# Hybrid encoder, two layers on one core: VectorE's waits for GpSimd counted for small operands, three projections in lockstep, memory keys 512 wide

## The chip, the core and the metric

The kernel runs on one NeuronCore of a Trainium2 chip. The metric is the time of one execution in microseconds (us) as the device reports it. Five engines work side by side, each with its own queue of instructions in fixed order: TensorE (PE in the profile, its weight loads PEld) multiplies matrices and writes PSUM; VectorE (DVE), ScalarE (ACT) and GpSimd (POOL) work on elements; SyncE (SP) issues most of the DMAs. An instruction waits on semaphores for what it needs, and all that stands behind it on its engine waits with it.

## The reference

An encoder of two layers over 512 tokens of width 1024, all in float32 (batch 1). Cut to what matters:

```python
for l in range(2):
    x = x + hybrid_mixer(rms_norm(x, norm_mix[l]), w_in[l], ...)      # 8 neighbourhood heads and 8 grouped-query heads
    x = x + memory_cross_attention(rms_norm(x, norm_mem_q[l]),        # 4 heads of width 128 over 256 memory tokens
                                   rms_norm(mem, norm_mem_kv[l]), ...)
    x = x + conv_ffn(rms_norm(x, norm_ffn[l]), ...)                   # 2 x 2816 wide, convolution of width 3, SwiGLU
return rms_norm(x, norm_final)
```

The mixer's one input projection gives queries, keys and values of both kinds of heads. In the grouped-query heads queries and keys are normalised per head, so the scores of a query are scaled by a factor of its own before the softmax. The memory keys are `rms_norm(mem) @ w_k`, 256 tokens by 512 columns, a product of its own in each layer.

## The kernel before

**Precision.** Every float32 operand of a matmul is kept as two parts, `hi` (rounded, by a copy on ScalarE) and `lo` (the difference, by a subtraction on GpSimd for weights or VectorE for activations). A product is three matmuls: hi by hi, hi by lo, lo by hi (`mm3`, line 609; `gemm_T`, 615). Norms are applied late: the operand is x times the gain, and the factor of each token is multiplied in after the projection.

**Tiles.** x lies transposed: `xT[0..7]` (line 621), eight tiles of 128 features by 512 tokens, 2048 bytes a row. Gains, convolution weights and biases lie in `par` (622). Weights come by DMA into `raw`, two buffers (`N_RAW`), or into the pool of 21 buffers tagged `r` where the plan says so (`"Dx"`, line 576); they are split into `hi` and `lo`, four buffers each. PSUM has eight banks: four tagged `mm` for projections, two `sc` for scores, two `tr` for transposes and small sums.

**The order of the work.** The function `encoder_kernel` doesn't issue anything itself. `Taped` engines record each call as a `Step` (line 73) on a `Tape`, with a cost from `Step.times`, the steps it needs, and whether it is `shared`, that is whether the model lets it and GpSimd's instructions exclude each other (line 97). `Tape.touch` notes for every tile who must wait for whom; line 178 makes each user of a tile need the tile's first user. `Tape.plan` (323) runs a list scheduler several times with three margins (`PLANS`), reckons due times backwards (`due`, 202), replays each order with random delays, and keeps the order with the best mean. `play` issues that order. In `run` (227) a shared step on VectorE is lengthened until the port is free (lines 293 to 296). Before the change a VectorE step is shared if it reads at least two operands of more than 16 columns and none of them lies in PSUM. All instructions are issued in `play`, so the profile gives line 355 for nearly everything; tiles tell them apart.

**Start.** `FIRST` (line 627) lists the first loads: x's chunks (integers) and pieces `(u, k0, k1)` of the first three projections' weights (u = 0, 1, 2; chunks k0 to k1), in pieces of two or four chunks. The eight gains of the first norm come as a DMA of their own on ScalarE's queue (628). `Norm.operand` (691) makes `hi` and `lo` of x times gain. `project_first` (853) then multiplies in an order that mixes the three projections, with the first two chunks of two of them written out by hand (864). The rest of `par` is loaded by `load_parameters` (644), after the projections.

**Grouped-query scores.** `gqa_scores` (1162) takes 128 queries of two heads. Per head j: two matmuls into a bank `sc`; VectorE reduces the row maximum, negated, into one column of `nmx`; VectorE multiplies it by the query's factor, one column `gr` (line 1173); ScalarE computes the exponential with that column as bias; GpSimd normalises; TensorE transposes. In the profile these are `s<-sc` (reduce), `s<-s,s` (multiply), `t<-sc,s,s` (exponential), `sc<-r,r` (scores). Only two banks hold scores, so a late exponential holds back the scores after the next. Projections, output products and the memory's keys and values are woven between as fillers (`attn_fill`, 1308).

**Memory keys.** `memory_prepare` (761) makes, for each of eight chunks of the memory, `hi` and `lo` of 256 columns, which lie side by side in a tile `mg`. `memory_keys` (1273) runs per head eight chunks of three matmuls of 256 columns into one half of a bank, then VectorE multiplies out of PSUM by `mem_rep` (the tokens' factors) into `u`, and `hi` and `lo` of that are made.

Of the kernel before, what the change touches and what calls it, by code (L numbers as in the profile page):

```python
# [19 lines left out]
P = 128  # L20
# [36 lines left out]
IN_PSUM = ("mm", "sc", "tr")  # L57
ASIDE = {"mm": 1, "r": 9, "t": 9, "s": 9}
# [14 lines left out]
class Step:  # L73
# [3 lines left out]
                 "opens", "tiles")  # L77

    def __init__(self, i, engine, name, call, args, kwargs):
        self.i, self.engine, self.name, self.call = i, engine, name, (call, args, kwargs)  # L80
        self.reads, self.writes = [], []
        for n, a in [*enumerate(args), *kwargs.items()]:
            if hasattr(a, "tensor") or type(a).__name__ == "Tile":
                a = a if hasattr(a, "ap") and not callable(a.ap) else a[:]
                (self.writes if n in (0, "out", "accum_out") else self.reads).append(a)
        self.needs, self.frees, self.opens, self.tiles, self.moved = set(), set(), [], [], 0
# [60 lines left out]
class Tape:  # L147
# [6 lines left out]
    def take(self, engine, name, call, args, kwargs):  # L154
        s = Step(len(self.steps), engine, name, call, args, kwargs)
        for a, w in [(a, False) for a in s.reads] + [(a, True) for a in s.writes]:
            if type(a.tensor).__name__ == "Tile":
                self.touch(s, a, w)
        s.needs.discard(s.i)
        for x in s.needs:  # L160
            self.steps[x].frees.add(s.i)
        self.steps.append(s)

    def touch(self, s, a, writes):
# [37 lines left out]
    def due(self, start, rank):  # L202

        later = [[] for _ in self.steps]
        for tag, tiles in self.opened.items():
            tiles = sorted(tiles, key=lambda t: rank[self.users[t][0]])
            for a, b in zip(tiles, tiles[self.bufs.get(tag, len(tiles)) :]):
                first = self.users[b][0]
                for x in self.users[a]:
                    if rank[x] < rank[first]:  # L210
                        later[x].append(first)
        at, now = [0.0] * len(self.steps), 0.0
        by_rank = sorted(self.steps, key=lambda s: rank[s.i])
        for s in by_rank:
            if s.engine == E_PE:
                now = start[s.i]
            at[s.i] = now + 30000.0 * (s.engine != E_PE)
        for s in reversed(by_rank):
            long = HANDOVER + (s.busy + LANDING + s.moved / BYTES_PER_NS if s.moved else s.length)
            for x in s.frees:  # L220
                same = self.steps[x].engine == s.engine and not s.moved
                at[s.i] = min(at[s.i], at[x] - (s.busy if same else long))
            for x in later[s.i]:
                at[s.i] = min(at[s.i], at[x] - long)
        return at

    def run(self, due, rank, patience, ahead, margin=0.0, aside={}, order=None, rng=None):
# [3 lines left out]
        todo = [len(s.needs) for s in steps]  # L231
# [28 lines left out]
        for _ in steps:  # L260
# [53 lines left out]
            for x in s.frees:  # L314
# [4 lines left out]
                if not todo[x]:  # L319
                    open_to[q.engine].append(x)  # L320
        return max(start), start, taken
# [128 lines left out]
def encoder_kernel(ctx: ExitStack, tc: tile.TileContext, t: dict, out: bass.AP):  # L450
# [170 lines left out]
    xT = [xpool.tile([P, S], F32, tag=f"x{c}", name=f"xT{c}") for c in range(KC)]  # L621
# [5 lines left out]
    FIRST = [0, (0, 0, 2), 1, (1, 0, 2), 2, (0, 2, 4), 3, (1, 2, 4), (2, 0, 4), 4, (0, 4, 8), 5, (1, 4, 8), (2, 4, 8), 6, 7]  # L627
    ACT.dma_start(par[:, 0, 0:8], t["par"][:, 0, 0:8])
    first_loads = []
    for n in FIRST:  # L630
        if isinstance(n, int):
            SP.dma_start(xT[n], t["xT"][n * P : (n + 1) * P, :])
            continue
        u, k0, k1 = n
# [3 lines left out]
        (ACT if u < 2 and k0 == 0 else SP).dma_start(raw[:, k0:k1], loads[0][1][:, k0:k1])  # L638
# [35 lines left out]
    class Norm:  # L674
# [16 lines left out]
        def operand(self, c, act=ACT, src=None, dve=DVE, hi_only=False, lo_only=False):  # L691
            src = xT[c] if src is None else src
            g = par[:, self.l, self.gcol + c : self.gcol + c + 1]
# [65 lines left out]
    mops = []  # L759

    def memory_prepare(l):

        mops.clear()
        raw = load_mem()
        yield
        for c in range(KC):
# [7 lines left out]
            mops.append((hi, lo))  # L774
            if c % 2 == 1:
                yield
# [38 lines left out]
    for n in FIRST:  # L815
# [3 lines left out]
        u, k0, k1 = n  # L819
        if u == len(ready):  # L820
            if plan[u][4][1:] == "r":
                ready.append((rtile((KC, P)), rtile((KC, P))))
            else:
                ready.append(tuple(wpool.tile([P, KC, P], F32R, tag=tag, name=nm(tag)) for tag in ("hi", "lo")))
        raw, (hi, lo) = raws[u], ready[u]
        k = slice(k0, k1)
# [7 lines left out]
        if k1 == KC:  # L834
# [6 lines left out]
    for l in range(DEPTH):  # L841
# [11 lines left out]
        def project_first():  # L853

            w, pms = {}, {}
            for u, k0, k1 in ((0, 0, 2), (1, 0, 2), (0, 2, 4), (1, 2, 4), (2, 0, 4), (0, 4, 6),
                              (1, 4, 6), (2, 4, 6), (0, 6, 8), (1, 6, 8), (2, 6, 8)):
                if u not in w:
                    w[u], pms[u] = get_w(NA_ORDER[u]), ps_s() if u < 2 else ps_mm()
                if (u, k0) == (0, 0):  # L860
                    continue
                if (u, k0) == (1, 0):

                    for v, a, b, k in ((0, 0, 0, 0), (0, 1, 0, 0), (0, 0, 0, 1), (0, 0, 1, 0), (1, 0, 0, 0), (1, 0, 0, 1),
                                       (0, 1, 0, 1), (0, 0, 1, 1), (1, 0, 1, 0), (1, 0, 1, 1), (1, 1, 0, 0), (1, 1, 0, 1)):
                        PE.matmul(pms[v], w[v][a][:, k], xg[k][b], start=(a, b, k) == (0, 0, 0), stop=False)
                    continue
                gemm_T(pms[u], w[u], xg, range(k0, k1), 0, KC - 1)
# [293 lines left out]
        def gqa_scores(u):  # L1162
# [110 lines left out]
        def memory_keys():  # L1273
            yield lambda: len(mops) == KC
            for h in range(4):
# [392 lines left out]
```

## Time and profile before

| | |
|---|---|
| timed runs, median of 3 | 1354.14 us (1353.62 to 1354.2) |
| profiled execution, whole | 1354.9 us |
| its span, first to last instruction | 1353.1 us |
| mean granted TensorE clock | 0.995 |
| instructions in the span | 18192 |
| HBM read, written | 125.65 MB, 2.10 MB |

A line of a group reads: source line, engine, operation, tiles written and read, shapes, count; then busy time in us, mean ns of one, idle time of the engine just before them, and after `<-` what ended it. In a timeline a row has start and length in us, and in square brackets the idle time before and its releaser. A row of the stages has the stretch, its length, the busy time and count of each engine, the granted clock, the DMA share and GB/s. A row of a tile has the count and the least, median and greatest duration in ns.

### The profile page before, as it was taken

Reading aid. Unit: us, or ns where it says so; the run is one execution under the profiler, and the core shown is the slowest. Engines: PE = TensorE matmul, PEld = TensorE weight load, DVE = VectorE, ACT = ScalarE, POOL = GpSimd, SP = SyncE. Lnnn points to the kernel's source line nnn. Section 1 sums busy time; section 2 is a strip of 40 time slices with the busy share of each in tenths; the row PEclk is TensorE's granted clock in tenths of the full one; section 3 lists DMA queues with packets and bytes.
Section 4 is the critical chain, followed back from the end, with each engine's and each line's share of the span. In section 5 each row is a group of like instructions: output and inputs, shape, how many; then the busy total and the mean of one; then the engine's idle time right before and its main releaser. Section 6 shows DMA issues by size and latency. Waiting matters only on the chain.

```text
span 1353.1 us, 18192 instructions
## 1 busy us (share of the span) xinstructions
PE 1332.5 (98%) x6620; PEld 1120.9 (83%) x6620; DVE 941.4 (70%) x1609; ACT 679.6 (50%) x1230; POOL 686.5 (51%) x475
## 2 busy tenths in 40 slices
PE   8999999999999999999999999999999999999997
PEld 7898788888888888888888987888888888888897
DVE  5679985676995388178435898856769925853884
ACT  6676676555443244233447767755634423432441
POOL 2474865727445444443636655756454544444451
PEclk9999999999999999999999999999999999999998
DMA  7761312323333332333265422133133333333331
GB/s 245 185 180 48 94 49 77 94 62 94 108 95 93 100 103 82 105 118 92 81 170 156 144 75 63 63 79 108 49 107 96 93 104 99 91 97 98 100 84 63
DMA packets 204504, 136.78 MB, mean 101 GB/s; under 512 B 5248, under 2 KB 193024, under 8 KB 204416
## 3 DMA queue, kind: packets, MB, share of 16 engines
q1 hardware_dynamic: 203312, 134.97, 34.2%
q8 instruction: 52, 0.85, 0.2%
q10 hardware_dynamic: 1104, 0.66, 0.2%
q14 instruction: 36, 0.29, 0.1%
HBM read 125.65 MB, written 2.10 MB: 94 GB/s over the span
## 4 chain that ended last, share of the span: by engine, by line
PE 88%; DVE 8%; ACT 2%; DMA 1%; issue 1%; POOL 0%; ACTq 0%; DVEq 0%
PE mm L355 79%; PE sc L355 5%; PE tr L355 4%; DVE s L355 3%; DVE t L355 2%; DVE r L355 1%; ACT t L355 1%; DVE xg L355 1%; DMA r<-r 0%; DVE xT L355 0%; ACT r L355 0%; DMA par<-in_par 0%; DVE sc L355 0%; DVE mm L355 0%; ACT xg L355 0%
## 5 line engine op out<-in xcount | busy, mean ns | idle before, releaser
L355 POOL TENSOR_TENSOR lo<-raw,hi 128x1024 fp32r<-128x1024 f32 (+2 forms) x268 | 506.8, 1902 | 505.9 <-ACT hi L355 467.8
L355 PE MATMUL mm<-xg,hi 128*128 128x512 f32 x1728 | 535.1, 390 | 0.0
L355 ACT CAST hi<-raw 128x512 fp32r<-128x512 f32 (+3 forms) x281 | 228.4, 831 | 313.4 <-PE mm L355 282.5
L355 PEld LDWEIGHTS mm<-xg,hi 128*128 128x128 f32 x1728 | 322.4, 188 | 65.2
L355 PE MATMUL mm<-xg,lo 128*128 128x512 f32 x864 | 336.4, 389 | 0.0
L355 PE MATMUL mm<-r,hi 128*128 128x512 f32 (+1 forms) x1144 | 333.8, 374 | 0.1
L355 DVE SCALAR_TENSOR_TENSOR t<-t,par,t 128x504 f32<-128x504 f32 (+1 forms) x352 | 247.7, 739 | 35.9 <-ACT t L355 32.2
L355 PEld LDWEIGHTS mm<-r,hi 128*128 128x128 f32 x1144 | 209.8, 189 | 38.7 <-DVE r L355 0.3
L355 PE MATMUL mm<-r,lo 128*128 128x512 f32 (+1 forms) x572 | 213.6, 373 | 0.0
L355 PEld LDWEIGHTS mm<-xg,lo 128*128 128x128 f32 x864 | 162.2, 188 | 33.7
L355 PEld LDWEIGHTS mm<-r,lo 128*128 128x128 f32 x572 | 107.8, 188 | 18.7
L355 DVE TENSOR_TENSOR xT<-xT,mm 128x512 f32<-128x512 f32 (+1 forms) x64 | 39.4, 618 | 118.3 <-PE mm L355 118.2
L355 PE MATMUL mm<-hi,xg 128*128 128x512 f32 (+1 forms) x384 | 107.9, 357 | 0.0
L355 POOL TENSOR_SCALAR t<-t,s 128x512 f32<-128x512 f32 (+1 forms) x112 | 67.6, 619 | 77.6 <-DVE s L355 70.9
L355 ACT ACTIVATE t<-sc,s,s 128x512 f32<-128x512 f32 (+1 forms) x96 | 67.9, 709 | 41.5 <-DVE s L355 41.2
L355 DVE TENSOR_TENSOR t<-mm,rep 128x512 f32<-128x512 f32 x88 | 60.0, 686 | 37.6 <-PE mm L355 22.3
L355 PE MATMUL sc<-r,r 128*128 128x256 f32 (+1 forms) x352 | 80.5, 341 | 5.6 <-ACT t L355 4.8
L355 ACT ACTIVATE t<-t,par 128x512 f32<-128x512 f32 x88 | 71.6, 814 | 28.0 <-DVE t L355 28.0
L355 DVE TENSOR_TENSOR t<-t,t 128x512 f32<-128x512 f32 (+1 forms) x68 | 76.4, 1123 | 8.6 <-ACT t L355 4.4
L355 DVE TENSOR_TENSOR r<-t,r 128x512 fp32r<-128x512 f32 (+1 forms) x52 | 71.5, 1375 | 13.5 <-ACT r L355 12.5
L355 PEld LDWEIGHTS mm<-hi,xg 128*128 128x128 f32 x384 | 68.6, 189 | 9.4
L355 PE MATMUL tr<-ident,t 128*128 128x128 f32 x488 | 70.8, 274 | 3.1 <-DVE r L355 1.6
(111 smaller groups left out, 1531.9 us busy)
## 6 DMA issues: line engine op xcount, KB each, us to landing
raw<-in_w_up SPq DMA_DIRECT2D x88, 512.0 KB, 3.8
raw<-in_w_in SPq DMA_DIRECT2D x33, 512.0 KB, 4.5
raw<-in_w_down SPq DMA_DIRECT2D x32, 448.0 KB, 3.8
raw<-in_w_mem_kv SPq DMA_DIRECT2D x16, 512.0 KB, 3.6
raw<-in_w_down SPq DMA_DIRECT2D x16, 512.0 KB, 4.0
r<-r SPq DMA_DIRECT2D x30, 256.0 KB, 3.6
r<-in_bias SPq DMA_DIRECT2D x16, 384.0 KB, 5.9
raw<-in_w_out SPq DMA_DIRECT2D x8, 512.0 KB, 3.3
```

Source lines behind the costliest of these rows:

```text
L355: call(*args, **kwargs)
```

## The change

Seven edits, in the order of the diff:

- `shared` on VectorE is no longer decided by width. Operations with two tensor inputs (`TWO_INPUTS`) are shared if their first and last input lie in SBUF, whatever their width; `tensor_scalar` and `tensor_copy` (`FAST`) are shared if they write more than four columns and both input and output lie in SBUF.
- Users of a tile that don't need the first user's data come after it in the order (`after`, `leads`) without waiting for its end.
- The first three projections all keep their raw weights in the `r` pool.
- x's chunks become 513 columns wide in the input and in SBUF; column 512 holds the first layer's first gain. The DMA of eight gains goes away, and `par` is loaded whole, in one DMA, after the projections.
- `FIRST` takes the weights in pieces of two chunks of all three projections, and `project_first` multiplies chunk by chunk, the three projections in turn.
- The one-column multiply of `gqa_scores` becomes a `tensor_scalar` that multiplies by the column and by 1.0.
- The memory keys' hi by hi and hi by lo become one matmul of 512 columns into both halves of a bank, lo by hi one of 256 into the first half; VectorE then copies the second half to SBUF, adds the first half, and multiplies by `mem_rep`.

Beside these, the reserve in SBUF for dynamic DMA is set to 1024 bytes. The diff, cut to its core:

```diff
+TWO_INPUTS = ("tensor_add", "tensor_sub", "tensor_mul", "tensor_tensor", "scalar_tensor_tensor")
+FAST = ("tensor_scalar", "tensor_copy")
...
-        wide = [a for a in self.reads if columns(a) > 16]
+        ends = self.reads[:: max(1, len(self.reads) - 1)] if name in TWO_INPUTS else self.reads[:1] + self.writes
         self.shared = engine == E_POOL or (
-            engine == E_DVE and len(wide) > 1 and all(tag_of(a.tensor) not in IN_PSUM for a in wide))
+            engine == E_DVE and (name in TWO_INPUTS or name in FAST and columns(self.writes[0]) > 4)
+            and all(tag_of(a.tensor) not in IN_PSUM for a in ends))
...
-            s.needs.add(self.users[t.name][0])
+            s.after.add(self.users[t.name][0])
...
+            for x in s.leads:
+                ready[x] = max(ready[x], t)
+                todo[x] -= 1
+                if not todo[x]:
+                    open_to[steps[x].engine].append(x)
...
-                eng = {("q", 0): "D", ("k", 0): "D", ("q", 1): "Dx"}.get((n, p), "P") if l == 0 else "P"
+                eng = {("q", 0): "Dx", ("k", 0): "Dx", ("q", 1): "Dx"}.get((n, p), "P") if l == 0 else "P"
...
-    xT = [xpool.tile([P, S], F32, tag=f"x{c}", name=f"xT{c}") for c in range(KC)]
+    xg0 = [xpool.tile([P, S + 1], F32, tag=f"x{c}", name=f"xT{c}") for c in range(KC)]
+    xT = [x[:, 0:S] for x in xg0]
...
-    FIRST = [0, (0, 0, 2), 1, (1, 0, 2), 2, (0, 2, 4), 3, (1, 2, 4), (2, 0, 4), 4, (0, 4, 8), 5, (1, 4, 8), (2, 4, 8), 6, 7]
-    ACT.dma_start(par[:, 0, 0:8], t["par"][:, 0, 0:8])
+    FIRST = [0, (0, 0), (1, 0), (2, 0), 1, 2, (0, 2), (1, 2), (2, 2), 3, 4, (0, 4), (1, 4), (2, 4), 5, 6, (0, 6), (1, 6), (2, 6), 7]
...
-        SP.dma_start(par[:, 0, 8:], t["par"][:, 0, 8:])
-        SP.dma_start(par[:, 1], t["par"][:, 1])
+        SP.dma_start(par, t["par"])
...
+            w = [get_w(NA_ORDER[u]) for u in range(3)]
+            pms = [ps_s(), ps_s(), ps_mm()]
+            for k in range(KC):
+                for u in range(3):
+                    gemm_T(pms[u], w[u], xg, [k], 0, KC - 1)
...
-                DVE.tensor_mul(nmx[:, c], nmx[:, c], gr[b][:, h])
+                DVE.tensor_scalar(nmx[:, c], nmx[:, c], gr[b][:, h], 1.0, op0=ALU.mult, op1=ALU.mult)
...
-                pm = ps_mm()[:, :MEMN]
-                w = get_w(("memk", h))
-                gemm_T(pm, w, mops, range(0, 4), 0, KC - 1)
-                yield
-                gemm_T(pm, w, mops, range(4, 8), 0, KC - 1)
+                pm = ps_mm().rearrange("p (n m) -> p n m", n=2)
+                wh, wl = get_w(("memk", h))
+                for k in range(KC):
+                    PE.matmul(pm, wh[:, k], both[k], start=k == 0, stop=False)
+                    PE.matmul(pm[:, 0], wl[:, k], mops[k][0], start=False, stop=k == KC - 1)
+                    if k == 3:
+                        yield
                 u = tmp((MEMN,))
-                DVE.tensor_mul(u, pm, mem_rep)
+                DVE.tensor_copy(u, pm[:, 1])
+                DVE.tensor_add(u, pm[:, 0], u)
+                DVE.tensor_mul(u, u, mem_rep)
...
-    nc = bacc.Bacc("TRN2", target_bir_lowering=False, num_devices=1)
+    nc = bacc.Bacc("TRN2", target_bir_lowering=False, num_devices=1, dynamic_dma_scratch_size=1024)
```

More of the change, by code (lines that the diff above doesn't have):

```diff
@@ L76 @@
     __slots__ = ("i", "engine", "name", "call", "reads", "writes", "busy", "length", "moved", "shared", "needs", "frees",
-                 "opens", "tiles")
+                 "after", "leads", "opens", "tiles")
     def __init__(self, i, engine, name, call, args, kwargs):
@@ L159, in take @@
         s.needs.discard(s.i)
+        s.after -= s.needs | {s.i}
         for x in s.needs:
             self.steps[x].frees.add(s.i)
+        for x in s.after:
+            self.steps[x].leads.add(s.i)
         self.steps.append(s)
@@ L230, in run @@
         steps = self.steps
-        todo = [len(s.needs) for s in steps]
+        todo = [len(s.needs) + len(s.after) for s in steps]
         start, ready, free = [-1.0] * len(steps), [0.0] * len(steps), [0.0] * 5
@@ L637, in encoder_kernel @@
         raw, loads = first_loads[u]
-        (ACT if u < 2 and k0 == 0 else SP).dma_start(raw[:, k0:k1], loads[0][1][:, k0:k1])
+        (ACT if u < 2 and k0 == 0 else SP).dma_start(raw[:, k0 : k0 + 2], loads[0][1][:, k0 : k0 + 2])
     ACT.copy(small(1), ones)
@@ L818, in encoder_kernel @@
             continue
-        u, k0, k1 = n
+        u, k0 = n
         if u == len(ready):
[L821 to L824, printed above, removed]
+            ready.append(tuple(wpool.tile([P, KC, P], F32R, tag=tag, name=nm(tag)) for tag in ("hi", "lo")))
         raw, (hi, lo) = raws[u], ready[u]
-        k = slice(k0, k1)
+        k = slice(k0, k0 + 2)
         if (u, k0) == (0, 0):
```

32 lines of the change are left out of this document (12 added, 20 removed).

## The prediction

> **What bounds the kernel now.** I read the page's first part, then the chain of work in order of time, then the busy time by stage, and last the timeline at the places where TensorE stood still.
>
> ```profile
> span 1353.1 us, 18192 instructions
> PE 1332.5 (98%) x6620; PEld 1120.9 (83%) x6620; DVE 941.4 (70%) x1609; ACT 679.6 (50%) x1230; POOL 686.5 (51%) x475
> ```
> ```profile
> 332.06 342.76 PE mm L355 x1512
> ...
> 1332.73 10.09 PE mm L355 x84
> ```
>
> TensorE is busy for 98% of the span, and in the long feed-forward stretches the chain is nothing but matmuls: 342.76 us / 1512 = 226.7 ns for one of 512 columns, 10.09 us / 84 = 120.1 ns for one of 256. Nothing that VectorE or GpSimd does there can move the end. What is left to gain are the start, the end, and the stages in which TensorE's busy time is less than the stretch (column order: length, PE, PEld, DVE, ACT, POOL, granted clock, DMA):
>
> ```profile
> 80.00:120.00 40.00, 38.21 (x262) 34.58 (x262) 34.20 (x91) 30.73 (x82) 26.57 (x31) 1.00 0.42 129
> 145.00:160.00 15.00, 13.33 (x65) 9.91 (x64) 13.86 (x27) 10.28 (x23) 11.07 (x12) 1.00 0.31 88
> 160.00:195.00 35.00, 33.95 (x191) 27.90 (x190) 30.58 (x63) 26.90 (x58) 22.53 (x25) 1.00 0.20 66
> 195.00:215.00 20.00, 19.65 (x129) 16.80 (x128) 17.26 (x35) 16.55 (x37) 13.42 (x15) 1.00 0.19 58
> 261.00:300.00 39.00, 38.55 (x212) 32.79 (x211) 24.49 (x65) 21.99 (x52) 12.15 (x6) 1.00 0.25 81
> 808.00:822.00 14.00, 12.26 (x53) 9.18 (x52) 11.93 (x23) 9.13 (x20) 9.52 (x10) 0.88 0.28 80
> 822.00:860.00 38.00, 37.05 (x208) 30.54 (x207) 33.21 (x68) 29.08 (x63) 23.90 (x27) 1.00 0.21 69
> 860.00:880.00 20.00, 19.66 (x130) 16.84 (x129) 17.21 (x35) 16.53 (x37) 14.34 (x15) 1.00 0.17 53
> 925.00:965.00 40.00, 39.55 (x217) 33.65 (x216) 24.77 (x65) 21.97 (x52) 12.27 (x6) 1.00 0.25 80
> ```
>
> The grouped-query stage (145 to 215 us, and 808 to 880 in the second layer) idles 1.67 + 1.05 + 0.35 + 1.74 + 0.95 + 0.34 = 6.10 us, and loses (1 - 0.88) x 14 = 1.7 us to a lower granted clock. The other three rows idle 1.79 + 0.45 + 0.45 = 2.69 us. So all that a better order could win back between start and end is 8.8 us idle and 1.7 us of clock. Now the deepest of these places, in the second layer's timeline:
>
> ```profile
> 812.29 1.30 DVE L355 TENSOR_TENSOR s<-s,s 128x1 f32<-128x1 f32 x1
> 812.29 2.50 POOL L355 TENSOR_TENSOR lo<-raw,hi 128x512 fp32r<-128x512 f32 x2
> ...
> 813.62 0.78 ACT L355 ACTIVATE t<-sc,s,s 128x512 f32<-128x512 f32 x1 [2.44 <-DVE s L355]
> ...
> 814.54 0.73 PE L355 MATMUL sc<-r,r 128*128 128x512 f32 x2 [1.35 <-ACT t L355]
> ```
> ```profile
> 151.71 0.73 PE L355 MATMUL sc<-r,r 128*128 128x512 f32 x2 [1.35 <-ACT t L355]
> ```
>
> A multiply of one column on VectorE takes 1.30 us because GpSimd holds a 1.25 us subtraction; the exponential behind it waits 2.44 us, the score bank stays full, and TensorE waits 1.35 us. The first layer waits as long in the same place (the second fence). In the second layer the granted clock of that stretch is 0.88, in the first it is 1.00.
>
> **The change part by part.**
>
> *The one-column multiply becomes a tensor_scalar.* How long each form takes on one column, and how often it is caught:
>
> ```profile
> L355 DVE TENSOR_TENSOR s<-s,s x64: 150/162/1299, 145.4 to 879.3; 128x1 f32<-128x1 f32 x64
> L355 DVE TENSOR_SCALAR s<-s,s x32: 201/206/217, 268.4 to 956.4; 128x1 f32<-128x1 f32 x32
> ...
> L355 DVE TENSOR_SCALAR s<-s,geps x8: 231/522/786, 121.8 to 806.5; 128x8 f32<-128x8 f32 x8
> ```
> ```profile
> L355 DVE TENSOR_TENSOR s<-s,s 128x1 f32<-128x1 f32 x64 | 30.9, 483 | 1.8
> ```
>
> Before, 64 multiplies have a median of 162 ns but a mean of 483: they stand 64 x (483 - 162) = 20.5 us behind GpSimd. The 32 one-column tensor_scalars of the memory attention never pass 217 ns. After, 64 x 206 = 13.2 us instead of 30.9: VectorE is freed of 17.7 us. What reaches the end: at 812.29 the multiply ends 1.30 - 0.21 = 1.1 us earlier, and so does the exponential, leaving 1.35 - 1.1 = 0.25 us; the next multiply behind it (0.59 us at 814.22) shrinks by 0.38 and takes that too. So 1.35 us per layer, 2.7 for both, and in the second layer the 1.7 us of clock, which I put down to the wait. Together **-4.4 us**. Next late there is the reduce of the scores itself, 0.68 us on VectorE. The bounds: 0 if the new form is caught as well (a piece that was never caught loses 44 ns, too little for TensorE), and -4.4 - 3.4 if the rest of the 6.10 goes too.
>
> The Trainium skill ("SBUF — State Buffer", section "Who interferes with whom") speaks against this: it lists tensor_scalar among the operations that can enter a two-port mode, and such an operation is locked out by GpSimd. The eight-column rows (to 786 ns) agree with it, the one-column rows do not: 32 of 32 are free. By the page alone this term would be 0.
>
> A second page bears on the 1.7 us. The Trainium skill ("TensorE: Matmul & The Clock Gate", Part 1) says that the clock falls back after an idle window of about 3.4 us; here it fell after a wait of 1.35 us in one layer and not in the other. By the page the 1.7 us would not hang on this wait, and the sum would be -4.6.
>
> *The planner's account.* It now reckons VectorE's waits for GpSimd for operations with two SBUF inputs of any width and for tensor_scalar and copies above four columns, and a tile's later users need only stand behind its first one in the order, no longer wait for its end. This issues nothing; it gives every engine another order from the first microsecond on. No row shows that order. Bounds: it wins at most the idle time that is left, 8.8 - 2.7 = 6.1 us; and it can open as much as it closes, two stalls of this kind with their lost clock, +4.4. I take 0: in the feed-forward stages, half of the span, the 1512 matmuls of the chain leave nothing to win, and for the rest I have no row that leans to either end.
>
> *Start.* The first gains travel as a 513th column of x, so the small load of parameters no longer stands before the first operand, and three projections advance together over x's chunks.
>
> ```profile
> xT<-in_xT SPq DMA_DIRECT2D x1, 256.0 KB, 3.1
> ```
> ```profile
> 5.15 0.72 ACT L355 ACTIVATE xg<-xT,par 128x512 fp32r<-128x512 f32 x1 [1.46 <-DMA par<-in_par]
> ...
> 5.93 0.50 PE L355 MATMUL sc<-xg,hi 128*128 128x512 f32 x1 [1.65 <-ACT xg L355]
> ...
> 7.06 1.54 PE L355 MATMUL sc<-xg,hi 128*128 128x512 f32 x4 [0.41 <-ACT xg L355]
> ```
> ```profile
> 7.50:10.00 2.50, 2.50 (x8) 1.99 (x7) 2.50 (x6) 2.50 (x5) 0.00 (x0) 0.54 1.09 341
> ```
>
> x's first chunk is issued at 0.72 us and lands after 3.1, so ScalarE could begin at 3.8 instead of 5.15; the first matmul moves from 5.93 to about 4.7. Behind it nine matmuls need only that one chunk, where before TensorE paused until 7.06 for the second. At the clock of that stretch (0.54) they last 9 x 0.227 / 0.54 = 3.8 us, ample for the second chunk. The ends are -2.1 (dense from 4.9 and not from 7.06) and +0.8 (three weight pieces with the first chunk are 640 KB where 384 sufficed, 0.8 us at the 341 GB/s of the row); I take **-1.0 us**, near the wait of 1.46 that goes. SyncE issues four pieces more, and x's rows become 2052 bytes, which no row shows; but all 3.6 MB are through in 10.8 us at 341 GB/s, by about 15, and the 72 matmuls (3.8 us for the first nine, 63 x 0.227) reach the last chunk at about 21: a cover of 6 us, value 0. The three projections' raw weights lie in other buffers, so the fourth's load can go earlier, and the two later parameter loads become one; nothing on TensorE waits for either before, 0. The smaller scratch buffer serves no queue that the page lists, 0.
>
> *Memory keys.* Per chunk two 256-column matmuls of the same weights become one of 512: 360.3 ns become 346.8. Times 64 (8 chunks, 4 heads, 2 layers): **-0.86 us**. VectorE pays for it:
>
> ```profile
> L355 DVE TENSOR_TENSOR t<-t,t 128x256 f32<-128x256 f32 x12 | 7.1, 593 | 2.4 <-ACT t L355 2.4
> ...
> L355 DVE TENSOR_TENSOR t<-mm,mem_rep 128x256 f32<-128x256 f32 x8 | 3.3, 412 | 0.0
> ...
> L355 DVE TENSOR_TENSOR t<-mm,t 128x256 f32<-128x256 f32 x4 | 1.7, 425 | 0.3
> ```
>
> One multiply out of PSUM (412 ns) becomes a copy (unseen at this size; about the 412 of the same read), an add (425) and a multiply of two SBUF tiles (593 with its waits): 1.02 us more, 8 times, 8.1 us. The keys are filler inside the grouped-query stage, where VectorE is 30.58 us busy of 35; the cover is the 17.7 us that the one-column multiplies give back in that stage. Value 0. Without that cover the score reduces queue behind them; price below.
>
> **Sum:** -4.4 - 1.0 - 0.86 = -6.3 us. The profiled execution took 1354.9 us (its span and 1.8 us around it), so 1348.6; it lies 0.8 above the median of the three timed runs, 1354.14, and on that the same sum gives **1347.8 us**.
>
> **The rivals**, on the median:
>
> - *The order gives it back* (chance 0.15). VectorE is busy for 85 to 92% of the grouped-query rows and two score banks tie reduce, exponential and scores together; a new order can put another late step where the multiply was. Price: the +4.4 above; 1354.14 - 1.9 = 1352.2. For it: the idle time that is left has many small owners. Against: what the old account missed is the very wait at 812.29.
> - *The tensor_scalar is caught too* (0.06): on one column it stands behind GpSimd in the grouped-query stage as the eight-column ones do, to 786 ns, and the exponential stays as late as it is. The 4.4 us are lost: -1.9, 1352.2. Against: the 217 ns. This is what the Trainium skill's "SBUF — State Buffer" makes of the change.
> - *VectorE pays for the keys where TensorE feels it* (0.16): slower. The multiply by the replicated row now reads two SBUF tiles and can stand behind GpSimd; the reduces of the next scores are queued behind it on VectorE, ScalarE's exponentials wait for those, TensorE for them. Eight such places at the price of the one that was measured, 1.35 us, are 10.8: -6.3 + 10.8 = +4.5, 1358.6. It makes the kernel slower by over 0.2% from (6.3 + 2.7) / 1.35, seven of eight, if all else comes as summed, and from four of eight if the order also gives its 4.4 back. For it: VectorE is the fullest engine beside TensorE there. Against: eight places, against 64 that are relieved.
> - *More goes* (0.16): the order wins two thirds of the 6.1 us left as well, -10.4, 1343.7.
>
> **How the numbers follow.** The forecast has 0.47. A measurement of this kernel tells about 0.2% (2.7 us) from no change. Faster by more: forecast but for 0.02 of it, and the last rival, 0.45 + 0.16 = 0.61. Within: 0.15 + 0.06 + 0.02 = 0.23. Slower: 0.16. The range goes from the last rival to past the two at 1352.2, up to where the third begins to show: 1343.0 to 1355.5, which leaves out about 0.2, nearly all above. The forecast's own range is 1345.0 to 1351.4.
>
> **What would show it.** One-column tensor_scalars between 200 and 220 ns in the grouped-query stage; no wait of over 0.6 us for the exponential there, and a granted clock of 1.00 in the second layer's; a first projection matmul before 5 us and none waiting until 25 us; 64 matmuls of 512 and 64 of 256 columns in the memory keys. It is wrong if TensorE's idle time in those stages stays near 6 us, if multiplies of two 256-column SBUF tiles stand in front of score reduces, or if the first matmuls wait for weights.

## The result, and the profile after

The changed kernel takes 1337.9 us, the median of four runs (1336.86 to 1338.56); the kernel before takes 1354.17 on the same chip. The ratio is 0.9876, with an interval of 0.9859 to 0.9893: **16.3 us faster**. The forecast of 1347.8 had the direction and less than half of the size, and 1337.9 lies below its range.

In the profile after, all instructions stand at line 369. The first rows of the page:

```profile
span 1335.8 us, 18093 instructions
...
PE 1323.1 (99%) x6556; PEld 1115.8 (84%) x6556; DVE 926.6 (69%) x1629; ACT 676.8 (51%) x1234; POOL 683.9 (51%) x475
```

TensorE's busy time went down by 1332.5 - 1323.1 = 9.4 us, though only 64 matmuls went, which by the prediction's own term are worth 0.86 us. So a busy time of TensorE contains something that isn't work. That is the thread of what follows. The chain of waits shows that a feed-forward stretch is what it was:

```profile
320.95 342.76 PE mm L369 x1512
```

The same stages after, 5 to 18 us earlier (same columns as before: length, PE, PEld, DVE, ACT, POOL, granted clock, DMA):

```profile
138.00:155.00 17.00, 16.79 (x87) 13.54 (x86) 16.23 (x35) 12.10 (x26) 14.89 (x15) 1.00 0.31 91
155.00:187.00 32.00, 32.00 (x173) 26.76 (x172) 27.75 (x63) 25.75 (x57) 22.83 (x26) 1.00 0.26 84
187.00:207.00 20.00, 20.00 (x117) 17.21 (x116) 18.91 (x44) 18.10 (x39) 14.46 (x15) 1.00 0.20 54
250.00:289.00 39.00, 39.00 (x215) 33.40 (x214) 24.01 (x66) 21.87 (x52) 12.53 (x6) 1.00 0.26 82
790.00:804.00 14.00, 13.47 (x62) 10.05 (x61) 12.98 (x27) 8.13 (x18) 11.30 (x11) 1.00 0.25 80
804.00:842.00 38.00, 37.56 (x202) 31.12 (x200) 33.83 (x72) 31.08 (x67) 28.00 (x31) 1.00 0.23 70
842.00:862.00 20.00, 19.67 (x114) 17.05 (x115) 18.43 (x42) 16.53 (x35) 14.01 (x16) 1.00 0.24 79
```

TensorE idles 0.21 + 0 + 0 + 0.53 + 0.44 + 0.33 = 1.5 us in the grouped-query stages, where it was 6.1, and the memory attention of the first layer (250 to 289) has no idle time left. The granted clock is 1.00 throughout.

VectorE's small operations after:

```profile
L369 DVE TENSOR_SCALAR s<-s,s x96: 198/214/217, 140.3 to 939.2; 128x1 f32<-128x1 f32 x96
...
L369 DVE TENSOR_SCALAR s<-s,geps x8: 230/546/1294, 131.0 to 802.4; 128x8 f32<-128x8 f32 x8
```

The 64 multiplies have joined the 32 one-column tensor_scalars, and none of the 96 takes more than 217 ns. The eight-column ones are caught as before.

The start, in the timeline:

```profile
3.70 0.72 ACT L369 ACTIVATE xg<-xT 128x512 fp32r<-128x512 f32 x1 [0.48 <-DMA xT<-in_xT]
...
4.51 0.53 PE L369 MATMUL sc<-xg,hi 128*128 128x512 f32 x1 [0.24 <-ACT xg L369]
...
5.23 0.40 ACT L369 CAST hi<-r 128x256 fp32r<-128x256 f32 x1 [0.80 <-DMA r<-in_w_in]
...
5.68 0.74 PE L369 MATMUL sc<-xg,hi 128*128 128x512 f32 x2 [0.64 <-ACT hi L369]
```

ScalarE begins at 3.70 instead of 5.15, the first matmul stands at 4.51 instead of 5.93. Then TensorE waits 0.64 us by its idle time for the second projection's weights, whose DMA landed at 5.2.

**Where the profile hides lost time.** The page's row of the largest group of matmuls:

```profile
L369 PE MATMUL mm<-xg,hi 128*128 128x512 f32 x1728 | 534.9, 390 | 0.0
```

One such matmul is recorded with 390 ns, but in the chain above they follow each other every 342.76 us / 1512 = 226.7 ns: records overlap by 163 ns. When a matmul starts late, the first 163 ns of the gap are covered by the record of the one before it and count as busy. So I left the busy time and went by starts. The loss of a stretch is its length less what its matmuls need back to back: 226.7 ns for 512 columns, 120 for 256, 109 for 128 or fewer (213 for each record of the identity matmuls at the start, which run at half speed, see the last section), all read from runs of matmuls without a gap. In us, from the trace's matmul records of one profiled execution each; the kernels of the last four columns are experiments told below:

| stretch | before | after | form only | account only | after, old multiply | after, old start |
|---|---|---|---|---|---|---|
| to the end of the first projections | 5.8 | 3.2 | 4.6 | 5.9 | 3.6 | 6.6 |
| from there to the first grouped-query scores | 3.3 | 1.5 | 2.8 | 3.3 | 1.4 | 3.3 |
| grouped-query stages, both layers | 15.6 | 5.3 | 4.2 | 11.1 | 16.1 | 5.3 |
| memory attention, both layers | 2.3 | 0.9 | 2.3 | 0.9 | 0.9 | 0.9 |
| all else, the tail above all | 10.4 | 10.1 | 10.5 | 9.9 | 10.5 | 10.8 |
| sum | 37.4 | 21.0 | 24.5 | 31.1 | 32.5 | 26.8 |

Beside the waits the columns hold some lost clock: half-speed matmuls in the first row (last section; 1.4 us before, 2.0 with the old start, at most 0.2 in the others), and a lowered clock in the third (1.6 before, 2.7 with the account alone). A profiled execution can also lie off the median of its kernel, by +0.7 us for before and -1.2 for the form alone, so that differences of two columns are known to about 2 us.

From before to after the loss shrinks by 16.4 us and the work itself by 0.9 (memory keys): together 17.3, the difference of the two spans. Of it 10.3 are in the grouped-query stages, where the idle time and the lowered clock had shown 7.8 us of loss and the starts show 15.6.

### The profile page after: what moved, and what is told of

It reads as the page before. It is cut to its first block, busy times and chain, and to the rows that moved or that the text cites. A ratio compares the mean times of both kernels' runs of the same rounds, so it can differ in the third digit from the quotient of the medians.

```text
span 1335.8 us, 18093 instructions
## 1 busy us (share of the span) xinstructions
PE 1323.1 (99%) x6556; PEld 1115.8 (84%) x6556; DVE 926.6 (69%) x1629; ACT 676.8 (51%) x1234; POOL 683.9 (51%) x475
## 4 chain that ended last, share of the span: by engine, by line
PE 91%; DVE 5%; ACT 2%; DMA 1%; issue 0%; POOL 0%; ACTq 0%; DVEq 0%
PE mm L369 81%; PE sc L369 6%; PE tr L369 4%; DVE t L369 2%; DVE s L369 1%; ACT t L369 1%; DVE r L369 1%; ACT r L369 0%; DMA r<-r 0%; DMA r<-in_w_in 0%; ACT hi L369 0%; DMA raw<-in_w_in 0%; DVE mm L369 0%; DVE xg L369 0%; DVE xT L369 0%
## 5 line engine op out<-in xcount | busy, mean ns | idle before, releaser
L369 ACT CAST hi<-raw 128x512 fp32r<-128x512 f32 (+2 forms) x276 | 226.3, 838 | 355.6 <-PE mm L369 318.7
L369 PEld LDWEIGHTS mm<-r,hi 128*128 128x128 f32 x1080 | 200.2, 188 | 39.7 <-DVE r L369 0.4
L369 DVE TENSOR_TENSOR r<-t,r 128x512 fp32r<-128x512 f32 (+1 forms) x52 | 82.4, 1585 | 14.6 <-ACT r L369 14.0
L369 PE MATMUL sc<-r,r 128*128 128x256 f32 (+1 forms) x352 | 74.8, 331 | 0.5 <-ACT t L369 0.4
L369 PEld LDWEIGHTS tr<-ident,t 128*128 128x128 f32 x488 | 58.2, 140 | 13.3 <-issue 2.2
```

The source lines that it names most:

```text
L369: call(*args, **kwargs)
```

## The experiments

Two theories stood against each other from the result on. By the first, the one-column multiply was worth far more than 4.4 us, in many small delays. By the second, it was worth what was forecast, and the new order won the rest. Experiments 1, 3, 4 and 5 were timed beside before on a chip where it takes 1354.15 us, 2, 7, 8 and 9 on one where it takes 1353.6, and 6, 10, 11 and 12 on one with 1353.86; after was not timed beside them, so a difference to its 1337.9 is known to about 1 us. The groups that tell most are these two, the score matmuls of the grouped-query heads before and after (count, busy us, mean ns of one, idle before):

```profile
L355 PE MATMUL sc<-r,r 128*128 128x512 f32 x128 | 46.1, 436 | 5.4 <-ACT t L355 4.8
```
```profile
L369 PE MATMUL sc<-r,r 128*128 128x512 f32 x128 | 40.9, 410 | 0.5 <-ACT t L369 0.4
```

**1. The form alone.** The kernel before with one line changed; the order of every engine stays the same.

```diff
-                DVE.tensor_mul(nmx[:, c], nmx[:, c], gr[b][:, h])
+                DVE.tensor_scalar(nmx[:, c], nmx[:, c], gr[b][:, h], 1.0, op0=ALU.mult, op1=ALU.mult)
```

> Kernel before, with the one edit that the multiply of gqa_scores is a tensor_scalar; the order on every engine stays that of before. Theory 1 (the caught multiply): the waits behind GpSimd made nearly every score matmul of the grouped-query stage late by less than the page counts as idle, so the form alone brings most of that stage back: 64 score matmuls a layer whose usual distance is 306 ns and becomes 230 to 240, 9 to 11 us in all, about 1344. Theory 2 (the order): the form is worth the 4.4 us of the prediction or less, about 1350 to 1351, the distance of the score matmuls stays near 300, and the rest of the gain comes from the new order.

Measured: 1343.15 us against 1354.15, ratio 0.992 (0.9904 to 0.9937), **-11.0 us**. No instruction was moved, so this is the price of the form itself. Its multiplies:

```profile
L355 DVE TENSOR_SCALAR s<-s,s x96: 201/214/216, 143.8 to 943.4; 128x1 f32<-128x1 f32 x96
```

Where it came from is read in the waits of the weight loads (PEld): in total, times, longest, all in us. Before, then with the form alone:

```profile
PEld sc L355 <- ACT t L355: 13.8, 23, 1.6
```
```profile
PEld sc L355 <- ACT t L355: 3.4, 8, 0.5
```

In these rows the wait for a free bank stands at the weight load of a score matmul. Weight loads are recorded with about 190 ns and fill less of the time, so their idle time shows what the matmuls' records cover: 13.8 us of waiting for exponentials where PE's column has 4.8. With the form alone 10.4 of the 13.8 are gone, close to the 11.0 measured. Going by starts, 60 of the 128 score matmuls before came late by over 20 ns, 43 of them by 163 ns or less. Over all 128, those that came early set against the late ones, the lateness is 9.9 us, of which 4.4 lay within the 163 ns that the record before covers; with the form alone 31 are late, and it is 1.5 us. The matmul after a late one comes late as well: the distances behind the 128 add up to 8.9 us over 226.7 ns each before, and to 5.1 with the form alone (0.2 of the 8.9 is lowered clock); their median went from 305 to 236 ns, as the first theory had it. How one such place looks before, in the timeline:

```profile
146.56 0.30 PEld L355 LDWEIGHTS sc<-r,r 128*128 128x128 f32 x2 [0.23 <-ACT t L355]
146.59 1.50 PE L355 MATMUL sc<-r,r 128*128 128x512 f32 x4
...
147.36 0.30 PEld L355 LDWEIGHTS sc<-r,r 128*128 128x128 f32 x2 [0.50 <-ACT t L355]
```

Four score matmuls, 1.50 us long, with no idle time on PE. Four without a gap take 3 x 0.227 + 0.39 = 1.07. The missing 0.43 us is to be seen only one row below: the second pair's weights waited 0.50 us for an exponential.

**2. The old multiply in the new order.** After, but the multiply is issued as a tensor_tensor while the planner still reckons a tensor_scalar, so that the order is after's.

```diff
-                DVE.tensor_scalar(nmx[:, c], nmx[:, c], gr[b][:, h], 1.0, op0=ALU.mult, op1=ALU.mult)
+                tape.take(E_DVE, "tensor_scalar", lambda o, a, g, one, op0, op1: nc.vector.tensor_mul(o, a, g),
+                          (nmx[:, c], nmx[:, c], gr[b][:, h], 1.0), dict(op0=ALU.mult, op1=ALU.mult))
```

> Kernel after, its order on every engine unchanged, but the one-column multiply is issued as the tensor_tensor of before. Theory 1 (the caught multiply): the multiplies stand behind GpSimd again, means near 480 ns, and the grouped-query stages lose most of what they won, 7 to 11 us, 1345 to 1349. Theory 2 (the order does it): the new order has room for the waits, and it costs 3 us or less, 1341 or less.

Measured: 1350.35 us, ratio to before 0.9976 (0.9965 to 0.9987); that is **12.4 us above after**, a little more than the 7 to 11 of the first theory. The waits of the weight loads are back, 12.4 us against 2.0:

```profile
PEld sc L369 <- ACT t L369: 12.4, 19, 1.6
```
```profile
PEld sc L369 <- ACT t L369: 2.0, 4, 0.6
```

(the first row with the old multiply, the second of after). The same place in both timelines, first with the old multiply:

```profile
805.38 1.29 DVE L1176 TENSOR_TENSOR s<-s,s 128x1 f32<-128x1 f32 x1
805.39 2.48 POOL L369 TENSOR_TENSOR lo<-raw,hi 128x512 fp32r<-128x512 f32 x2
806.71 0.78 ACT L369 ACTIVATE t<-sc,s,s 128x512 f32<-128x512 f32 x1 [2.44 <-DVE s L1176]
...
807.63 0.73 PE L369 MATMUL sc<-r,r 128*128 128x512 f32 x2 [1.35 <-ACT t L369]
```
```profile
801.38 0.21 DVE L369 TENSOR_SCALAR s<-s,s 128x1 f32<-128x1 f32 x1
801.39 2.52 POOL L369 TENSOR_TENSOR lo<-raw,hi 128x512 fp32r<-128x512 f32 x2
801.63 0.78 ACT L369 ACTIVATE t<-sc,s,s 128x512 f32<-128x512 f32 x1 [1.36 <-DVE s L369]
...
802.55 0.73 PE L369 MATMUL sc<-r,r 128*128 128x512 f32 x2 [0.26 <-ACT t L369]
```

GpSimd does the same beside both; the multiply takes 1.29 or 0.21 us, and TensorE waits 1.35 or 0.26. Experiments 1 and 2 take the form out of either order and agree: 11.0 and 12.4. The first theory stands.

**3. The account alone.** Before with the new `shared` rule and the new edges between a tile's users; multiply, start and keys are the old ones.

```diff
-        wide = [a for a in self.reads if columns(a) > 16]
+        ends = self.reads[:: max(1, len(self.reads) - 1)] if name in TWO_INPUTS else self.reads[:1] + self.writes
...
-            s.needs.add(self.users[t.name][0])
+            s.after.add(self.users[t.name][0])
```

> Kernel before, with the planner's new account alone (shared by place of the operands, and users that only follow a tile's first user); the multiply stays a tensor_tensor. Theory 1: the multiply is still caught, though the planner now sees it; at most 3 to 5 us, about 1350. Theory 2: the order that knows the waits brings the gain, 8 us or more, about 1346 or less, with hardly any caught multiply left.

Measured: 1348.39 us, ratio 0.9958 (0.9943 to 0.9973), **-5.8 us**, between the two theories; the multiplies are caught still, as the first had it:

```profile
L369 DVE TENSOR_TENSOR s<-s,s x64: 139/258/1353, 144.8 to 876.9; 128x1 f32<-128x1 f32 x64
```

But the order now places other work around them: the table's column has 4.5 us less in the grouped-query stages, though its profiled execution ran part of them at a lower clock (0.77 in this row; the half clock lasted from 159.78 to 166.61 us), and 1.4 less in the memory attention.

```profile
155.00:170.00 15.00, 11.34 (x49) 8.84 (x47) 11.62 (x22) 8.76 (x20) 9.21 (x9) 0.77 0.27 75
```

**4. The start alone.** Before with x's 513th column, the new `FIRST`, the lockstep, the single load of `par`, the three raw weights in the `r` pool and the smaller scratch buffer.

```diff
-    ACT.dma_start(par[:, 0, 0:8], t["par"][:, 0, 0:8])
...
+            for k in range(KC):
+                for u in range(3):
+                    gemm_T(pms[u], w[u], xg, [k], 0, KC - 1)
```

> Kernel before, with the start alone (gains in x's 513th column, pieces of two chunks, three projections in turn). Theory 1: 2.5 us, about 1351.6, because the first matmuls come at 4.5 us and TensorE's clock is never halved between 7 and 11 us. Rival: the start is worth the 1.0 us that was forecast, about 1353, and the halved clock comes back, since it fell by chance.

Measured: 1354.81 us, ratio 1.0008 (0.9999 to 1.0017): nothing gained, where the two expectations were 2.5 and 1.0. The half clock came back, as the rival had it: nine matmuls in a row ran so. By starts, and without matmuls at half speed (last section), the loss to the end of the first projections is 2.8 instead of 3.1 us, counted from the first identity matmul; 0.7 us more is won up to the first grouped-query scores. But the order changed down to the second layer: the first layer's grouped-query stage loses 8.0 instead of 7.2, and the second layer's neighbourhood attention 1.4 instead of 0.7. The second layer's grouped-query stage loses 6.5 instead of 8.4, but 1.6 of that is the lowered clock in before's execution.

**5. The keys alone**, and **6. after without them.** The diff is that of `memory_keys`, put into before and taken out of after:

```diff
+                    PE.matmul(pm, wh[:, k], both[k], start=k == 0, stop=False)
+                    PE.matmul(pm[:, 0], wl[:, k], mops[k][0], start=False, stop=k == KC - 1)
...
+                DVE.tensor_copy(u, pm[:, 1])
+                DVE.tensor_add(u, pm[:, 0], u)
+                DVE.tensor_mul(u, u, mem_rep)
```

> Kernel before, with the memory keys alone at 512 columns. Theory 1: 0.9 us of matmuls, about 1353.3, if VectorE's eight-microsecond bill is hidden. Rival: in the order of before, where VectorE is pressed, the added operations delay the reduces and the gain is lost or turned, 1354 to 1357.

> Kernel after with the memory keys as before. Theory: 0.9 us of matmuls and nothing else, 1338.8. Rival: the added work of VectorE costs, and without it the time is at or under 1337.5.

Measured: keys alone 1352.37 us, 0.9986 (0.9977 to 0.9996), -1.8, an interval that takes in the 0.9 of the matmuls; after without them 1338.55, 0.9884 (0.9868 to 0.9901), 0.65 above after, which four runs each don't separate. Neither direction shows a cost. VectorE pays more than forecast, in after:

```profile
L369 DVE TENSOR_TENSOR t<-t,mem_rep 128x256 f32<-128x256 f32 x8 | 9.0, 1126 | 0.0
...
L369 DVE COPY t<-mm 128x256 f32<-128x256 f32 x8 | 3.3, 416 | 0.1
```

The multiply of two SBUF tiles takes 1126 ns on average instead of 593: the three of the eight that begin while GpSimd stands idle take 405 to 417 ns, the five that begin while it works 1127 to 2803. With the copy, and an add of 418 (the 128x256 form `t<-mm,t` of the same view), less the 412 that went, that is 1.55 us more, 8 times, 12.4 us. TensorE doesn't feel it.

**7. After without the start.**

```diff
-    xg0 = [xpool.tile([P, S + 1], F32, tag=f"x{c}", name=f"xT{c}") for c in range(KC)]
-    xT = [x[:, 0:S] for x in xg0]
+    xT = [xpool.tile([P, S], F32, tag=f"x{c}", name=f"xT{c}") for c in range(KC)]
+    ACT.dma_start(par[:, 0, 0:8], t["par"][:, 0, 0:8])
```

> Kernel after without the new start (loads, gains and first projections as before). Theory: the start is worth 1.4 us of matmuls that no longer stand still, and the rest of what the first 25 us show is a clock that is halved in some executions and not in others: 1339.3. Rival: the start is worth 2.5 us, 1340.4; other rival, from the start alone, which gained nothing: 1338.

Measured: 1342.73 us, ratio 0.9915 (0.9899 to 0.9932), 4.8 above after and above all three expectations. By the table the profiled execution loses 3.4 more before the end of the first projections, but 2.0 of these are ten half-speed matmuls, which another execution need not have, and 1.8 more between them and the first grouped-query scores; one place of the latter, where TensorE stands for the norm's factors:

```profile
27.74 0.49 PE L369 MATMUL tr<-ident,s 128*128 128x128 f32 x2 [0.79 <-POOL s L369]
```

**8. and 9. After without the one or the other half of the account.**

```diff
-            engine == E_DVE and (name in TWO_INPUTS or name in FAST and columns(self.writes[0]) > 4)
-            and all(tag_of(a.tensor) not in IN_PSUM for a in ends))
+            engine == E_DVE and len(wide) > 1 and all(tag_of(a.tensor) not in IN_PSUM for a in wide))
```

> Kernel after, but the planner decides by width which operations wait for GpSimd, as before. Theory: once the multiply cannot be caught, the other small operations matter little, and the account is worth 0 to 1.5 us: 1338 to 1339.5. Rival: the account is worth what it brought by itself, about 5 us: 1343.

```diff
-            s.after.add(self.users[t.name][0])
+            s.needs.add(self.users[t.name][0])
```

> Kernel after, but each user of a tile waits for the end of the tile's first user in the plan, as before. Theory: this edge lets second halves be planned 0.1 to 0.2 us earlier and moves nothing that TensorE waits for, 0 to 1 us: 1338 to 1339. Rival: it is the part that closes the gaps in the projections before the grouped-query stage (about 1.8 us of loss less there): 1340.

Measured: with the old `shared` rule 1342.37 us, 0.9918 (0.9903 to 0.9932), 4.5 above after; with the old edges 1341.01, 0.9906 (0.9891 to 0.9921), 3.1 above. Each half is worth something in the whole, nearer to the rival's expectation than to the theory's in both. By starts, beside the other draws of experiment 10, the old rule loses 4.4 us more: 2.2 in the grouped-query stages and 1.6 in the second layer's neighbourhood attention. The old edges lose 2.7 more, 2.3 of it before the first grouped-query scores, where 0.6 is a first chunk of x that came late in this execution.

**10. and 11. Other orders under the same account.** Either other random draws in the planner's replays, or other margins. With the draws another instruction than in after stands in 7% of TensorE's places and 15% of VectorE's, with the margins in 9% and 26%.

```diff
-                under = [self.run(None, rank, (0.0,) * 5, 0, order=r[2], rng=np.random.default_rng(k)) for k in range(3)]
+                under = [self.run(None, rank, (0.0,) * 5, 0, order=r[2], rng=np.random.default_rng(k + 10)) for k in range(3)]
```

> Kernel after with other random delays in the planner's replay, which picks another, nearly equal order. If an order's own luck is small, 1337 to 1339; if the 3 to 5 us that single parts seemed to be worth are such luck, 1340 to 1343.

```diff
-PLANS = [((60.0, 300.0, 300.0, 300.0, 0.0), 300, margin, ASIDE, 3) for margin in (40.0, 80.0, 120.0)]
+PLANS = [((60.0, 300.0, 300.0, 300.0, 0.0), 300, margin, ASIDE, 3) for margin in (60.0, 100.0, 140.0)]
```

> Kernel after with the planner's three margins at 60, 100 and 140 ns in place of 40, 80 and 120: a wholly other order under the same account. Small luck of an order: 1336 to 1340. Large luck: 1341 or more, or under 1335.

Measured: 1337.3 us (0.9877, 0.9862 to 0.9892) and 1337.24 (0.9878, 0.9863 to 0.9892). Three orders from one account lie within 0.7 us. So the 4.5 and 3.1 of experiments 8 and 9 are more than these draws differ by: an order planned with the new account is better, as far as one order of each old half can tell.

**12. Nine identity matmuls ahead instead of six**, after otherwise, to keep TensorE busy until the first operand is there.

```diff
-N_RAW, N_W, AHEAD, AHEAD_HELD, N_WARM, N_LATE, N_FIRST = 2, 4, 2, 5, 6, 4, (12, 22)
+N_RAW, N_W, AHEAD, AHEAD_HELD, N_WARM, N_LATE, N_FIRST = 2, 4, 2, 5, 9, 4, (12, 22)
```

> Kernel after, order unchanged, with nine and not six matmuls on the identity ahead of the first projection (1.3 us more of work that nothing reads). Theory: the half-speed stretch of 1.2 to 2.2 us that 7 of the 10 executions looked at show in their first 13 us follows the standstill of 0.4 and 0.9 us around the first real matmul; filled, it does not come: no half-speed matmul before 25 us, times closer together, 1336.5 to 1338. Rival: it comes by chance whatever is done, and the filler delays the first projection: 1338 to 1339.

Measured: 1337.84 us (1337.73 to 1338.11), ratio 0.9882 (0.9867 to 0.9897): no gain over after's 1337.9. The profiled execution has no half-speed matmul ahead of the projections' end but the identity ones, and the four times lie closer together than after's (0.4 us, not 1.7), as the theory had it; but after's profiled execution has none either, so this doesn't test the theory (the last section has more of it). No experiment gave a version that beats after by more than the runs scatter.

## Why the prediction was right or wrong

*The multiply: right in mechanism, wrong in size.* Forecast -4.4, measured -11.0 in the old order and 12.4 in the new. The new form isn't caught, 96 of 96 times. At the place that was worked out the first part of the working holds: 1.1 us earlier, and 0.25 left by the prediction, 0.26 in after and 0.27 with the form alone. That the next multiply takes this rest too doesn't hold; it stays. What failed is the step "So all that a better order could win back between start and end is 8.8 us idle and 1.7 us of clock". It took TensorE's idle time for all of its lost time, and so priced two waits of 1.35 us and nothing else; the lower bound of -7.8 came from the same count. The runs showed 60 late score matmuls, 43 of them late by no more than the 163 ns that the record before covers. The row that would have told it was there to be read: 13.8 us of waits on the weight loads. And 64 multiplies that lose 20.5 us on VectorE, in a stage where scores, reduce and exponential form a chain over two banks, should have been asked how much of the 20.5 reaches TensorE: over half did.

*The clock: that the 1.7 us hung on the wait isn't borne out.* With the old multiply in the new order the second layer has the wait of 1.35 us, and in the stretch around it TensorE idles 3.2 us, yet the granted clock is 1.00:

```profile
800.00:822.00 22.00, 18.83 (x90) 13.51 (x89) 20.18 (x38) 13.60 (x31) 15.53 (x17) 1.00 0.26 72
```

The Trainium skill ("TensorE: Matmul & The Clock Gate", Part 1), which asks for an idle window of about 3.4 us, would not have booked the 1.7 us here, and this run speaks for it. It doesn't explain why the clock fell in before, where no wait for an exponential was over 1.6 us, nor why it fell for 6.83 us with the account alone, where TensorE had waited 1.75 us shortly before and stood in a wait of 1.85 us; that stays open. Nor does before always fall: 12 of the 36 executions of it that ran beside the experiments have a mean granted clock of 0.998, which leaves no room for it. (An estimate: 5 us of half clock at the end, the least of the 14 profiled executions, and one fall of 3.41 us give 0.997.) The prediction took the clock of one execution for that of the kernel.

*The account: 0 was wrong.* Alone it is worth -5.8; that this is near its bound of -6.1 is chance, since the bound counted idle time alone, and the mean clocks of its four executions, 0.994 to 0.996, are among the lowest on record. In the memory attention it won 1.4 us, where the idle time had shown 0.45 a layer. The reason given for 0, that no row leaned to either end, overlooked that the multiplies' 20.5 us of waits were unknown to the old planner, which is a row that leans.

*The start: about right at its own place, not in what it does to the rest.* The first matmul stands at 4.51 us (4.7 forecast). Without the share of half-speed matmuls (below), the loss up to the end of the first projections is about 4.4 us before (5.8 - 1.4) and 3.2 after: -1.2 against -1.0. With the old account it is -0.3 (experiment 4). But the second part, "none waiting until 25 us", failed: TensorE waits at 5.68 for the weights, as the prediction had listed among the signs of being wrong. And taking the start out of after costs 4.8, putting it into before brings nothing: its worth depends on the account that orders the work behind it.

*The keys: right.* -0.86 forecast, 0.65 by taking them out (within the scatter), and the work shrank by 0.9 in the trace. VectorE's part costs 12.4 us instead of 8.1 and is hidden. The cover named for it wasn't even needed: in experiment 5 the old multiplies gave no time back, and the keys cost nothing either.

*The rivals.* "VectorE pays for the keys" is refuted by experiments 5 and 6: the multiply by `mem_rep` does stand behind GpSimd, but taking it out gains nothing. "The order gives it back" is refuted by 3, 10 and 11. "The tensor_scalar is caught too" is refuted by 217 ns; the Trainium skill ("SBUF — State Buffer", "Who interferes with whom") lists the operation as one that can be locked out, and here that holds for eight columns, to 1294 ns, not for one. Another page of the Trainium skill ("VectorE: DVE Perf Modes", "Mode 2×_2P") says that the second port reads the second half of the operand; one column has no second half, which would fit, but no run tests it. "More goes" had the sign of the error but got its 4.1 us from the wrong place, the idle time.

*What doesn't add up.* The four parts alone give -11.0 - 5.8 + 0.7 - 1.8 = -17.9 us, the whole change -16.3. After without the start (1342.73) is about where the form alone is (1343.15). The form's share is settled by two experiments; how the rest, about 5 us, divides between account and start isn't, since each needs the other. Four runs of a kernel also can't tell 1 or 2 us of half-speed start from a part's worth.

## What to carry to other kernels

Where an instruction's record is longer than the distance to the next one, idle time is only the part of a stall that exceeds the overlap: take the start-to-start distances, or the idle time of the weight loads, before calling idle time the most that can be won. A delay that repeats 64 times in a chain over two buffers is priced by how often the next link is late at all, not by the two places where it is worst. And a change to a planner's account and a change to what it plans are tried together and apart, since one can hide the other.

## What the runs showed of the hardware

TensorE runs the start at half speed, for longer than a stage row shows. In after with the old edges (experiment 9), the timeline and then the stage row around it:

```profile
7.21 0.63 PE L358 MATMUL sc<-xg,lo 128*128 128x512 f32 x1
7.63 0.63 PE L358 MATMUL sc<-xg,hi 128*128 128x512 f32 x1
8.06 0.63 PE L358 MATMUL sc<-xg,lo 128*128 128x512 f32 x1
```
```profile
6.70:9.10 2.40, 2.40 (x7) 1.83 (x6) 1.78 (x4) 2.40 (x5) 0.00 (x0) 1.00 1.06 351
```

These matmuls follow each other every 0.43 us instead of 0.227, TensorE is busy all the time, and the granted clock says 1.00. But the trace of this execution holds no clock record before 9.31 us, and the row counts such time as full. The record at 9.31 says full clock, and from there the distances are 0.22 to 0.24 us. In experiment 12 the identity matmuls stand 213 ns apart up to 4.50 us and 112 from 4.64 on; the first clock record there is at 4.54. In the other 13 executions, too, the identity matmuls behind the first stand 213 ns apart, where other matmuls of 128 columns need 109. So each execution ran at half speed from its first matmul to its first clock record, which stands at 4.3 to 5.0 us in five of the 14 (after at 4.64) and at 9.0 to 12.4 us in nine. In before it fell once more, from 7.72 to 11.13 us, and that is the 0.54 which its row had shown.

In 9 of the 14 profiled executions, that of before among them, 6 to 11 matmuls in a row between 6 and 12.5 us run so, each 0.2 us late: 1.2 to 2.2 us; in the others at most one. After and the kernel of experiment 12 had none. It belongs to the execution at least as much as to the kernel: other draws (experiment 10), whose first 32 matmul records have after's order, had it. The Trainium skill ("TensorE: Matmul & The Clock Gate", Part 1) gives 426.7 ns for 512 columns with the clock halved and says that the number of such matmuls varies from run to run; the distances here, 426 to 427 ns, and the 0 to 11 matmuls agree. The same part of the Trainium skill says that recorded clock events were seen to be unreliable; in these 14 executions the records and the distances agree. So the first microseconds of two single profiles can't be compared without counting these matmuls.
